# Float32 products of a mixed block in another order: whole-array, half-array and quarter-array products grouped, S5's in-block products moved ahead of its scan

## The chip, the core and the metric

The kernel runs on one core of a Trainium2 chip. The metric is the device time of one launch in microseconds, as the median of several launches. TensorE does the matrix products; VectorE, ScalarE and GpSimd do the rest; SyncE's queue (SP) issues the DMA transfers.

## The reference

Two transformer-like blocks on a sequence of 512 tokens and a width of 1024, all in float32. The first block (two layers of attention and gated products) isn't touched. The second block first mixes its input by three branches whose gated sum goes on, and the change lies in this mix:

```python
def rwkv7_mix(...):      # 8 heads of 64
    def step(S, inp):
        r_t, w_t, k_t, v_t, kk_t, a_t = inp
        sa = jnp.einsum('bhvk,bhk->bhv', S, -kk_t)
        S = (S * w_t[:, :, None, :] + sa[..., None] * (kk_t * a_t)[:, :, None, :]
             + v_t[..., None] * k_t[:, :, None, :])
        return S, jnp.einsum('bhvk,bhk->bhv', S, r_t)

def s5_mix(...):         # 32 groups of 16 channels, 64 complex states each
    _, _, s_re, s_im = lax.associative_scan(_complex_affine_combine, elems, axis=1)
    y = (einsum('blgn,gcn->blgc', s_re, c_re) - einsum('blgn,gcn->blgc', s_im, c_im) + d * uf)
    ...                  # gelu, and a gate by y @ w_glu

def gla_mix(...):        # 4 heads, chunks of 64 tokens
    att = where(mask, einsum('bhncd,bhnsd->bhncs', q_dec, k_inv), 0.0)
    o = einsum('bhncs,bhnse->bhnce', att, v)
    u = einsum('bhncd,bhnce->bhnde', k * exp(b_last - b), v)
    ...                  # S_prev: the state before each chunk, by a scan over chunks
    o = o + einsum('bhncd,bhnde->bhnce', q_dec, S_prev)
```

After the mix come a product with w_out, a cross attention and a convolutional feed-forward part, which are not touched.

## The kernel before

The large projections (x by a weight matrix) are computed as three products of rounded halves: `L282`, `L283` and `L284` in the helper `mm3`, with results in banks called `ps_mm`. Weights come by DMA as `wraw`, ScalarE casts the upper part `wh` at `L312`, and VectorE forms the lower part `wl` at `L314`. Each is one record in the trace. The small products of the mix are plain float32, and each takes two records, since the array passes over them twice. Their banks are called `ps_ch` (RWKV) and `ps_si` (S5 and GLA).

A tensor with 128 channels holds two heads of 64, one in rows 0 to 63 (`UP`) and one in rows 64 to 127 (`DOWN`). A product thus uses the whole array (128 rows by 128 columns, written 128*128 in the profile), a row half (64*128), a column half (128*64) or a quarter (64*64).

RWKV is done in chunks of 64 tokens for four tiles `t` of two heads, in the order 2, 3, 0, 1. `rwkv_a` makes gates and decays (with two products of rank 64 at its start). `rwkv_lower` makes a triangular matrix (`L1482`); its in-chunk inverse, for all four tiles together, is made by `rwkv_invert`, a chain of 30 steps on VectorE (`L1504`, `L1505`), whose result is copied (`L1512`) and goes through DRAM (`L1516`, `L1517`, read back at `L1472`). `rwkv_b` continues with `L1541` and `L1551`, and then

- E and F, per head e: four whole-array products (`L1630`) and four column-half products (`L1631`), one of each in turns into one bank, then the evacuation of that bank;
- G and h, per half of a chunk pair: 24 quarter products (`L1654` to `L1656`) in one bank, heads in turns.

S5 runs in two halves of eight group pairs. Each half makes its injection (`L2105`), rotates and scans it on VectorE and GpSimd (`L2111` to `L2125`), and then, for each group pair, adds two in-block products (`L2147`, matrices `mid`) and four products with the scan's result (`L2151`). The results go to DRAM (`L2092`) and come back for the gated output (`L2165`, then the products by `w_glu`).

GLA runs for two pairs of heads `j`: projections q (evacuated at `L1762`), k (`L1767`) and v, the state updates u (`L1791`), the in-chunk scores (`L1804`), and the output o, per head four products over whole blocks (`L1814`), each followed by two row-half products with the state (`L1817`).

Every part is a Python generator. `yield x` tells the code that builds the program how much TensorE work, in microseconds by its own reckoning, the step has issued, or, as a negative number, how long the next step has to wait for other engines. The builder then puts in projection products and steps of other parts (`kit.fill`), and so sets the order on every engine's queue. A change in a `yield`, or in what stands between two, moves work nearby.

## Time and profile before

| | |
|---|---|
| median of 3 runs | 2738.64 us (2735.85 to 2743.93) |
| profiled execution, its own time | 2742.08 us |
| its span, first to last instruction | 2740.3 us |
| TensorE busy | 2630.8 us, 96 % |
| VectorE, ScalarE, GpSimd busy | 58 %, 43 %, 19 % |
| mean granted TensorE clock | 0.968 |
| second block's mix | 1526 to 2197 us |

The profile was taken in one execution, so its rows add up to its own time. A share of busy time is a mean over stages with different limits. The granted clock is that of TensorE, as a part of 2.4 GHz; a mean between 0.5 and 1 is a mixture of the two levels, 1.2 and 2.4 GHz. The time from one record's start to the next one's says more of what a product costs than its busy time, as products overlap.

### The profile page before, as it was taken

The numbers are of one execution on the slowest core, as the hardware profiler recorded it, in microseconds if no ns is written. First come the engines' busy times: TensorE is split into PE (matmuls) and PEld (weight loads), VectorE is DVE, ScalarE is ACT, GpSimd is POOL, SyncE is SP. The second block draws the span as 40 slices with busy tenths as digits, with TensorE's granted clock in tenths as the row PEclk, the third lists the DMA queues.
The fourth block names the chain that finished last, engine by engine and source line by source line (L and its number), as shares of the span: only waits on it lengthen the run. The fifth ranks groups of instructions, "written<-read, shape, count | busy, mean of one in ns | idle before, by whom it ended". The sixth has DMA issues, their size and how long they took to land. (4 is left out here: it accounts for less than half of the span.)

```text
span 2740.3 us, 37093 instructions
## 1 busy us (share of the span) xinstructions
PE 2630.8 (96%) x13432; PEld 2124.6 (78%) x13432; DVE 1594.6 (58%) x3076; ACT 1182.4 (43%) x2209; POOL 519.7 (19%) x439
## 2 busy tenths in 40 slices
PE   8999999999999998999999889799999999999998
PEld 6668778888776787887877667677878788888886
DVE  5686654344457867966345667635453656774673
ACT  4576543233445755332333231425223445543443
POOL 5325021011210121243112331111130300100001
PEclk9999999999999999999999998799989999999999
DMA  4112223333422131334434343422212433233332
GB/s 153 36 50 90 61 89 93 100 99 91 128 72 62 55 101 55 116 118 139 142 89 135 108 171 107 108 70 83 66 44 72 119 116 102 81 97 95 100 93 70
DMA packets 172520, 258.51 MB, mean 94 GB/s; under 512 B 42528, under 2 KB 60832, under 8 KB 172320
## 3 DMA queue, kind: packets, MB, share of 16 engines
q1 hardware_dynamic: 172336, 256.13, 30.4%
q8 instruction: 106, 1.74, 0.3%
q14 instruction: 78, 0.64, 0.1%
HBM read 234.04 MB, written 22.15 MB: 93 GB/s over the span
## 5 line engine op out<-in xcount | busy, mean ns | idle before, releaser
L312 ACT CAST wh<-wraw 128x512 fp32r<-128x512 f32 (+1 forms) x777 | 473.4, 613 | 920.9 <-PE ps_mm L283 646.1
L314 DVE TENSOR_TENSOR wl<-wraw,wh 128x512 fp32r<-128x512 f32 (+1 forms) x691 | 488.1, 709 | 346.0 <-ACT wh L312 334.0
L282 PE MATMUL ps_mm<-xs,wh 128*128 128x512 f32 x1544 | 626.7, 406 | 8.9 <-ACT wh L312 7.9
L284 PE MATMUL ps_mm<-xs,wl 128*128 128x512 f32 x1544 | 615.6, 399 | 7.7 <-DVE wl L314 6.9
L283 PE MATMUL ps_mm<-xs,wh 128*128 128x512 f32 x1544 | 616.0, 399 | 2.0 <-DVE xs L264 1.9
L282 PEld LDWEIGHTS ps_mm<-xs,wh 128*128 128x128 f32 x1544 | 295.6, 191 | 76.4 <-ACT wh L312 8.5
L284 PEld LDWEIGHTS ps_mm<-xs,wl 128*128 128x128 f32 x1544 | 295.6, 191 | 75.4 <-DVE wl L314 9.6
L283 PEld LDWEIGHTS ps_mm<-xs,wh 128*128 128x128 f32 x1544 | 295.5, 191 | 66.1 <-DVE xs L264 5.7
L448 POOL TENSOR_TENSOR acc<-acc,za 128x512 f32<-128x512 f32 x59 | 82.0, 1389 | 730.4 <-ACT za L444 729.0
L282 PE MATMUL ps_mm<-za,wh 128*128 128x512 f32 x460 | 183.4, 399 | 5.5 <-ACT za L248 5.5
L284 PE MATMUL ps_mm<-za,wl 128*128 128x512 f32 x460 | 182.0, 396 | 4.1 <-DVE wl L314 4.1
L283 PE MATMUL ps_mm<-za,wh 128*128 128x512 f32 x460 | 180.9, 393 | 0.2 <-DVE za L245 0.2
L314 POOL TENSOR_TENSOR wl<-wraw,wh 128x512 fp32r<-128x512 f32 x86 | 112.4, 1316 | 308.5 <-ACT wh L312 303.7
L1193 POOL TENSOR_TENSOR za<-za,za 128x512 f32<-128x512 f32 x44 | 60.0, 1363 | 461.2 <-ACT za L1192 461.2
L284 PEld LDWEIGHTS ps_mm<-za,wl 128*128 128x128 f32 x460 | 87.3, 190 | 24.8 <-DVE wl L314 4.5
L282 PEld LDWEIGHTS ps_mm<-za,wh 128*128 128x128 f32 x460 | 87.5, 190 | 24.4 <-ACT za L248 6.4
L282 PE MATMUL ps_mm<-zb,wh 128*128 128x512 f32 (+1 forms) x284 | 100.6, 355 | 4.4 <-ACT zb L248 4.4
L245 DVE TENSOR_TENSOR za<-ps_tr,za 128x512 fp32r<-128x512 f32 (+3 forms) x152 | 84.6, 558 | 32.9 <-ACT za L248 31.8
L283 PEld LDWEIGHTS ps_mm<-za,wh 128*128 128x128 f32 x460 | 87.2, 189 | 20.4 <-DVE za L245 1.0
L283 PE MATMUL ps_mm<-zb,wh 128*128 128x512 f32 (+1 forms) x284 | 97.3, 343 | 0.1
L284 PE MATMUL ps_mm<-zb,wl 128*128 128x512 f32 (+1 forms) x284 | 97.3, 343 | 0.0
L468 POOL TENSOR_TENSOR rs<-sm,neghalf 128x4 f32<-128x4 f32 (+2 forms) x32 | 44.9, 1404 | 267.4 <-DVE sm L467 267.4
(592 smaller groups left out, 4918.2 us busy)
## 6 DMA issues: line engine op xcount, KB each, us to landing
wraw<-w_gu SPq DMA_DIRECT2D x176, 256.0 KB, 2.7
wraw<-w_dn SPq DMA_DIRECT2D x96, 256.0 KB, 2.6
wraw<-w_up SPq DMA_DIRECT2D x88, 256.0 KB, 2.6
wraw<-w_gate SPq DMA_DIRECT2D x48, 256.0 KB, 2.7
wraw<-w_dn SPq DMA_DIRECT2D x48, 192.0 KB, 2.3
dram<-za SPq DMA_DIRECT2D x26, 256.0 KB, 2.2
zc<-dram SPq DMA_DIRECT2D x26, 256.0 KB, 4.5
wraw<-w_cd SPq DMA_DIRECT2D x24, 256.0 KB, 2.7
```

What stands on the lines that cost most here:

```text
L245: self.nc.vector.tensor_tensor(lo, src, hi.bitcast(F32), op=ALU.subtract)
L282: mm(out, ah, bh, start=start, stop=False, **kw)
L283: mm(out, ah, bl, start=False, stop=False, **kw)
L284: mm(out, al, bh, start=False, stop=stop, **kw)
L312: self.nc.scalar.copy(hl[0], raw)
L314: eng.tensor_tensor(hl[1], raw, hl[0].bitcast(F32), op=ALU.subtract)
L448: self.nc.gpsimd.tensor_tensor(self.acc[0], self.acc[0], sq, op=ALU.add)
L468: self.nc.gpsimd.tensor_tensor(r, ms, self.neghalf[:, :n], op=ALU.pow)
L1193: nc.gpsimd.tensor_tensor(a, a, st["rb"], op=ALU.mult)
```

## The change

The products keep their operands and sums; their order changes, and with it the split into yields.

- `rwkv_a`: the two low-rank products of a tile, one in the upper and one in the lower rows, are issued in turns.
- `rwkv_b`, E and F: both heads get their bank first, the eight whole-array products stand together, then the eight column-half products of the two heads in turns, then both evacuations.
- `rwkv_b`, G and h: one loop over both halves and both heads, so that four quarters stand in turns; the yield between the halves is gone.
- GLA: u's two halves in turns with one yield; o in two banks at once, whole-array products together, then the row halves of the two heads in turns, and one yield of 2 more ahead of the evacuations.
- S5: the in-block products of a half stand ahead of the scan, with their four matrices in the loads made ahead (eleven tiles instead of seven); behind the scan only the scan's products remain, with a yield of 0.5 after every second group pair instead of 1.2 after each.

```diff
@@ -1405,5 +1405,7 @@
         w_up = self.narrow(I["w_up"][:, 0, t * 128 : t * 128 + 128])
-        for rows_, bias, out in ((UP, "w0", sw), (DOWN, "a0", a)):
-            p = kit.bank(CH)
-            kit.mm3(p, [z[rows_] for z in w_up], [z[rows_] for z in self.lora], True, True)
+        ps = [kit.bank(CH) for _ in range(2)]
+        for i, (x, y) in enumerate(((0, 0), (0, 1), (1, 0))):
+            for p, rows_ in zip(ps, (UP, DOWN)):
+                nc.tensor.matmul(p, w_up[x][rows_], self.lora[y][rows_], start=i == 0, stop=i == 2)
+        for p, bias, out in zip(ps, ("w0", "a0"), (sw, a)):
             nc.scalar.activation(out, p, AF.Sigmoid, bias=self.vec(bias, t))
@@ -1624,9 +1626,13 @@
         E, F = kit.f(), kit.f()
-        for e in range(2):
-            p = kit.bank(CH)
-            own, oth = slice(e * 64, e * 64 + 64), slice(64 - e * 64, 128 - e * 64)
+        ps = [kit.bank(CH) for _ in range(2)]
+        for e, p in enumerate(ps):
             for b in range(4):
                 s = slice(b * 128, b * 128 + 128)
-                mm(p[:, s], pair(wu, e, b), bb[e][:, s], start=True, stop=True)
-                mm(p[oth, s], head(st["vt"], e, b), lk[e * 4 + b][:, 128:256], start=False, stop=True, skip_group_check=True)
+                mm(p[:, s], pair(wu, e, b), bb[e][:, s], start=b == 0, stop=True, skip_group_check=True)
+        for b in range(4):
+            s = slice(b * 128, b * 128 + 128)
+            for e, p in enumerate(ps):
+                mm(p[halves[1 - e], s], head(st["vt"], e, b), lk[e * 4 + b][:, 128:256], start=False, stop=True, skip_group_check=True)
+        for e, p in enumerate(ps):
+            own, oth = halves[e], halves[1 - e]
             for b in range(4):
@@ -1645,13 +1651,12 @@
                                     st["pc"][own].unsqueeze(2).broadcast_to([64, 8, 64]), op=ALU.mult)
-        for half in range(2):
-            p = kit.bank(CH)
-            rows_ = slice(half * 64, half * 64 + 64)
-            for b in range(4):
-                for e in range(2):
-                    own = slice(e * 64, e * 64 + 64)
-                    w, u = (pair(wu, e, b)[rows_, o : o + 64] for o in (e * 64, 64 - e * 64))
-                    g_, h_ = p[own, b * 64 : b * 64 + 64], p[own, 256 + b * 64 : 320 + b * 64]
-                    mm(g_, w, head(st["bt"], e, b)[rows_], start=True, stop=True)
-                    mm(h_, head(st["bt"], e, b)[rows_], u, start=True, stop=False)
-                    mm(h_, head(st["kt"], e, b)[rows_], head(st["vt"], e, b)[rows_], start=False, stop=True)
+        ps = [kit.bank(CH) for _ in range(2)]
+        four = [(p, rows_, e) for p, rows_ in zip(ps, halves) for e in range(2)]
+        for b in range(4):
+            g_, h_ = slice(b * 64, b * 64 + 64), slice(256 + b * 64, 320 + b * 64)
+            own_, oth_ = ([pair(wu, e, b)[:, o : o + 64] for e, o in enumerate(os)] for os in ((0, 64), (64, 0)))
+            bt, kt, vt = ([head(st[n], e, b) for e in range(2)] for n in ("bt", "kt", "vt"))
+            for c_, x, y, start, stop in ((g_, own_, bt, True, True), (h_, bt, oth_, True, False), (h_, kt, vt, False, True)):
+                for p, rows_, e in four:
+                    mm(p[halves[e], c_], x[e][rows_], y[e][rows_], start=start, stop=stop)
+        for half, p in enumerate(ps):
             for e in range(2):
@@ -1786,5 +1791,4 @@
             u = [kit.bank(SI) for _ in range(2)]
-            for half in range(2):
-                rows_ = slice(half * 64, half * 64 + 64)
-                for b in range(4):
+            for b in range(4):
+                for half, rows_ in enumerate((UP, DOWN)):
                     for e in range(2):
@@ -1792,3 +1796,3 @@
                            st["kd"][rows_, b * 128 + e * 64 : b * 128 + e * 64 + 64], vb(b, e)[rows_], start=True, stop=True)
-                yield 1.2
+            yield 1.2
             yield -7.0
@@ -1808,11 +1812,13 @@
             yield -3.0
-            for e in range(2):
-                rows_, a = (UP, DOWN)[e], as_[e]
-                o = kit.bank(SI)
+            os = [kit.bank(SI) for _ in range(2)]
+            for e, o in enumerate(os):
                 for b in range(4):
                     w = slice(b * 128, b * 128 + 128)
-                    mm(o[:, w], vb(b, e), a[:, w], start=True, stop=True)
-                    for ch in (2 * b, 2 * b + 1):
-                        w = slice(ch * 64, ch * 64 + 64)
-                        mm(o[:, w], by4(s[ch // 4])[rows_, ch % 4], st["q"][rows_, w], start=False, stop=True, skip_group_check=True)
+                    mm(o[:, w], vb(b, e), as_[e][:, w], start=b == 0, stop=True, skip_group_check=True)
+            for ch in range(8):
+                w = slice(ch * 64, ch * 64 + 64)
+                for o, rows_ in zip(os, (UP, DOWN)):
+                    mm(o[:, w], by4(s[ch // 4])[rows_, ch % 4], st["q"][rows_, w], start=False, stop=True, skip_group_check=True)
+            yield 2.0
+            for o in os:
                 sq, y = kit.f(), kit.f()
@@ -2086,3 +2092,4 @@
             return [kit.load("", src=self.s5_tab[i, half]) for i in range(3)], [
-                kit.load("", src=self.s5_in[o, half * 2 + g]) for o in range(2) for g in range(2)]
+                kit.load("", src=self.s5_in[o, half * 2 + g]) for o in range(2) for g in range(2)], [
+                kit.load("", src=self.s5_mid[:, 16 * half + 4 * g : 16 * half + 4 * g + 4, :].rearrange("p g x -> p (g x)")) for g in range(4)]
 
@@ -2096,3 +2103,3 @@
         for half in range(2):
-            (cs, sn, m8), w_in = ahead
+            (cs, sn, m8), w_in, mids = ahead
             kit.need(*moves[2 * half : 2 * half + 2])
@@ -2114,3 +2121,12 @@
             tt(b, inj[0], sn, op=ALU.mult)
-            yield -4.0
+            yield -2.0
+
+            ps = [kit.bank(SI), kit.bank(SI)]
+            for g in range(8):
+                for e, p in enumerate(ps):
+                    c = (g % 2 * 2 + e) * 128
+                    mm(p[:, g * BLKS : g * BLKS + BLKS], mids[g // 2][:, c : c + 128], block(2 * (8 * half + g) + e),
+                       start=g == 0, stop=True, skip_group_check=True)
+                if g % 4 == 3:
+                    yield 0.9
             pt(x, x, a, op=ALU.add)
@@ -2129,8 +2145,5 @@
                 ahead = half_loads(1)
-            ps = [kit.bank(SI), kit.bank(SI)]
-            mids, cos = {}, {}
+            cos = {}
 
             def out_loads(gp):
-                if gp < 8 * half + 8 and gp % 2 == 0:
-                    mids[gp // 2] = kit.load("", src=self.s5_mid[:, 2 * gp : 2 * gp + 4, :].rearrange("p g x -> p (g x)"))
                 if gp < 8 * half + 8 and gp // 3 not in cos:
@@ -2142,12 +2155,8 @@
                 out_loads(gp + 1)
-                mid, co = mids[gp // 2], cos[gp // 3]
-                p = [z[:, g * BLKS : g * BLKS + BLKS] for z in ps]
-                for e in range(2):
-                    c = (g % 2 * 2 + e) * 128
-                    mm(p[e], mid[:, c : c + 128], block(2 * gp + e), start=True, stop=True)
                 c = gp % 3 * 144 + 16
-                for w, s in zip(co, (sr, si)):
-                    for e, rows_ in enumerate((UP, DOWN)):
-                        mm(p[e][:, 1:], w[rows_, c : c + 128], v8(s)[rows_, g, : BLKS - 1], start=False, stop=True, skip_group_check=True)
-                yield 1.2
+                for w, s in zip(cos[gp // 3], (sr, si)):
+                    for p, rows_ in zip(ps, (UP, DOWN)):
+                        mm(p[:, g * BLKS + 1 : g * BLKS + BLKS], w[rows_, c : c + 128], v8(s)[rows_, g, : BLKS - 1], start=False, stop=True, skip_group_check=True)
+                if g % 2:
+                    yield 0.5
             for e in range(2):
```

The program order shows what the planner makes of it. A row has the line, the operation, output and operands with buffer numbers, and the size; "x4" stands for four alike. Line numbers of the changed kernel are its own: what was `L1630` and `L1631` is `L1631` and `L1635` there, and `L1482` or later lines are shifted by 2 to 13.

On TensorE, E and F of the first tile (t=2), before, for one head (bank 16924); `za` are operands in SBUF:

```order
L1630 MATMUL ps_ch_16924<-za_16620,za_16869 128x128
L1631 MATMUL ps_ch_16924<-za_16521,za_16704 64x128
L1630 MATMUL ps_ch_16924<-za_16620,za_16869 128x128
L1631 MATMUL ps_ch_16924<-za_16521,za_16704 64x128
L1630 MATMUL ps_ch_16924<-za_16620,za_16869 128x128
L1631 MATMUL ps_ch_16924<-za_16558,za_16704 64x128
L1630 MATMUL ps_ch_16924<-za_16620,za_16869 128x128
L1631 MATMUL ps_ch_16924<-za_16558,za_16704 64x128
```

The same place on TensorE in the changed kernel, both heads (banks 17066 and 17067):

```order
L1631 MATMUL ps_ch_17066<-za_16784,za_17039 128x128 x4
L1631 MATMUL ps_ch_17067<-za_16801,za_17052 128x128 x4
L1635 MATMUL ps_ch_17066<-za_16686,za_16898 64x128
L1635 MATMUL ps_ch_17067<-za_16694,za_16898 64x128
L1635 MATMUL ps_ch_17066<-za_16686,za_16898 64x128
L1635 MATMUL ps_ch_17067<-za_16694,za_16898 64x128
L1635 MATMUL ps_ch_17066<-za_16738,za_16898 64x128
L1635 MATMUL ps_ch_17067<-za_16772,za_16898 64x128
L1635 MATMUL ps_ch_17066<-za_16738,za_16898 64x128
L1635 MATMUL ps_ch_17067<-za_16772,za_16898 64x128
```

Whole-array and column-half products alternated, with the other head's eight products elsewhere; now they stand in two blocks for both heads.

On TensorE, the output of S5's second half, before. The rows ahead are GLA's k projection (`ps_mm_16235`), those behind GLA's v:

```order
L284 MATMUL ps_mm_16235<-xs_14112,wl_16232 128x512
L2147 MATMUL ps_si_16006<-x_14829,zc_16008 128x64
L2147 MATMUL ps_si_16007<-x_14829,zc_16008 128x64
L2151 MATMUL ps_si_16006<-zc_15949,zc_16010 128x63
L2151 MATMUL ps_si_16007<-zc_15949,zc_16010 128x63
L2151 MATMUL ps_si_16006<-zc_15952,zc_16012 128x63
L2151 MATMUL ps_si_16007<-zc_15952,zc_16012 128x63
...
L2151 MATMUL ps_si_16006<-zc_15952,zc_16074 128x63
L2151 MATMUL ps_si_16007<-zc_15952,zc_16074 128x63
L282 MATMUL ps_mm_16310<-wh_16288,xs_13673 128x256
```

The same place in the changed kernel; the rows ahead are GLA's gate projection of 16 channels, those behind GLA's q projection (`ps_mm_16169`, weights `wh_16159` and `wl_16160`):

```order
L284 MATMUL ps_mm_16086<-xs_14112,wl_16083 16x512
L2159 MATMUL ps_si_15939<-zc_15903,zc_16016 128x63
L2159 MATMUL ps_si_15940<-zc_15903,zc_16016 128x63
L2159 MATMUL ps_si_15939<-zc_15906,zc_16018 128x63
L2159 MATMUL ps_si_15940<-zc_15906,zc_16018 128x63
...
L2159 MATMUL ps_si_15939<-zc_15906,zc_16058 128x63
L2159 MATMUL ps_si_15940<-zc_15906,zc_16058 128x63
L282 MATMUL ps_mm_16169<-xs_13673,wh_16159 128x512
L283 MATMUL ps_mm_16169<-xs_13674,wh_16159 128x512
L284 MATMUL ps_mm_16169<-xs_13673,wl_16160 128x512
```

The block shrank from 48 products to 32, since 16 in-block products went ahead of the scan, and GLA's q and k projections, which stood ahead of the block, stand behind it.

On VectorE, the end of the inversion, before; `wl` rows are the lower parts of weights (16226 and 16232 for GLA's k, 16289 and 16295 for v):

```order
L1505 TENSOR_TENSOR zc_15749<-zc_15749,zc_15750 128x16x8
L314 TENSOR_TENSOR wl_16226<-wraw_16223,wh_16225 128x512
L1504 TENSOR_TENSOR zc_15750<-zc_15748 128x54
L314 TENSOR_TENSOR wl_16232<-wraw_16229,wh_16231 128x512
L1505 TENSOR_TENSOR zc_15748<-zc_15748,zc_15750 128x6x9
L314 TENSOR_TENSOR wl_16289<-wraw_16286,wh_16288 128x512
...
L1504 TENSOR_TENSOR zc_15750<-zc_15749 128x30
L1505 TENSOR_TENSOR zc_15749<-zc_15749,zc_15750 128x30
L1741 TENSOR_TENSOR zc_16141<-ps_mm_16104,acc_14154 16x512
L314 TENSOR_TENSOR wl_16295<-wraw_16292,wh_16294 128x512
```

The end of the inversion on VectorE in the changed kernel (`wl_16160` and `wl_16166` for GLA's q, 16210 and 16216 for k, 16273 for v; `L1506` and `L1507` are the inversion, `L1746` is what was `L1741`):

```order
L1506 TENSOR_TENSOR zc_15794<-zc_15793 128x30
L1507 TENSOR_TENSOR zc_15793<-zc_15793,zc_15794 128x30
L314 TENSOR_TENSOR wl_16160<-wraw_16157,wh_16159 128x512
L1746 TENSOR_TENSOR zc_16123<-ps_mm_16086,acc_14154 16x512
L314 TENSOR_TENSOR wl_16166<-wraw_16163,wh_16165 128x512
L245 TENSOR_TENSOR zc_16079<-zc_16123,zc_16078 16x512
L314 TENSOR_TENSOR wl_16210<-wraw_16207,wh_16209 128x512
L314 TENSOR_TENSOR wl_16216<-wraw_16213,wh_16215 128x512
L314 TENSOR_TENSOR wl_16273<-wraw_16270,wh_16272 128x512
```

The lower parts of the weights for q and k, which were formed inside the inversion, are formed behind its last step.

## Rows read from the trace of the kernel before

**Rows 1.** The page: span, busy times, and granted clock in 40 slices.
```profile
span 2740.3 us, 37093 instructions
...
PE 2630.8 (96%) x13432; PEld 2124.6 (78%) x13432; DVE 1594.6 (58%) x3076; ACT 1182.4 (43%) x2209; POOL 519.7 (19%) x439
...
PEclk9999999999999999999999998799989999999999
```

**Rows 2.** Windows of the mix: busy us and counts by engine, granted clock, DMA.
```profile
core 0: us, PE busy (x) PEld busy (x) DVE busy (x) ACT busy (x) POOL busy (x), PEclk, DMA share, GB/s
1970.00:2003.00 33.00, 32.27 (x173) 25.57 (x174) 5.99 (x18) 5.76 (x10) 5.61 (x7) 0.64 0.14 42
1700.00:1716.00 16.00, 13.05 (x101) 11.55 (x100) 14.53 (x45) 2.30 (x5) 0.00 (x0) 0.68 0.09 14
1716.00:1750.00 34.00, 22.63 (x138) 19.49 (x137) 15.54 (x21) 15.83 (x25) 6.84 (x5) 0.65 0.49 114
1526.00:2197.00 671.00, 622.08 (x3694) 496.64 (x3693) 366.85 (x674) 233.95 (x400) 156.17 (x126) 0.91 0.31 94
```

**Rows 3.** TensorE's timeline: a whole-array run, and row halves in turns.
```profile
1872.37 0.39 PE L284 MATMUL ps_mm<-xs,wl 128*128 128x512 f32 x1
1872.60 0.27 PE L1574 MATMUL ps_ch<-za,za 128*128 128x128 f32 x1
...
1873.41 0.48 PE L282 MATMUL ps_mm<-xs,wh 128*128 128x512 f32 x1
...
1741.04 1.16 PE L1482 MATMUL ps_ch<-za,za 64*128 64x128 f32 x16
1742.13 0.39 PE L282 MATMUL ps_mm<-wh,xs 128*128 128x256 f32 x1
```

**Rows 4.** TensorE's timeline, E and F of one head, first rows and next.
```profile
1806.52 0.39 PE L1630 MATMUL ps_ch<-za,za 128*128 128x128 f32 x2
1806.84 0.43 PE L1631 MATMUL ps_ch<-za,za 128*64 128x128 f32 x2
...
1809.18 0.43 PE L1631 MATMUL ps_ch<-za,za 128*64 128x128 f32 x2
```

**Rows 5.** TensorE's timeline, GLA's o of one head: first, last and next.
```profile
1809.55 0.38 PE L1814 MATMUL ps_si<-zc,zc 128*128 128x128 f32 x1
...
1813.24 0.38 PE L1817 MATMUL ps_si<-zc,zc 64*128 64x64 f32 x2
1813.56 0.50 PE L282 MATMUL ps_mm<-zc,wh 128*128 128x512 f32 x1
```

**Rows 6.** TensorE's timeline, G and h of one half: first and next.
```profile
1826.34 0.27 PE L1654 MATMUL ps_ch<-za,za 64*64 64x64 f32 x1
...
1828.05 0.50 PE L282 MATMUL ps_mm<-xs,wh 128*128 128x512 f32 x1
```

**Rows 7.** TensorE's timeline, S5's output: one group pair, then the second half.
```profile
1661.39 0.33 PE L2147 MATMUL ps_si<-x,zc 128*128 128x64 f32 x2
...
1662.46 0.50 PE L282 MATMUL ps_mm<-xs,wh 128*128 128x512 f32 x1
...
1700.11 0.55 PE L2147 MATMUL ps_si<-x,zc 128*128 128x64 f32 x4
...
1715.36 0.55 PE L282 MATMUL ps_mm<-wh,xs 128*128 128x256 f32 x1 [2.95 <-DVE zc L1741]
```

**Rows 8.** TensorE's timeline, E and F of another head, first and next.
```profile
1986.90 0.63 PE L1630 MATMUL ps_ch<-za,za 128*128 128x128 f32 x2
...
1992.12 0.47 PE L1654 MATMUL ps_ch<-za,za 64*64 64x64 f32 x2
```

**Rows 9.** VectorE's timeline: the inversion's first and last steps, what follows, S5's read-back.
```profile
1673.98 0.17 DVE L1504 TENSOR_TENSOR zc<-zc 128x14 f32<-128x14 f32 x1
...
1714.36 0.19 DVE L1505 TENSOR_TENSOR zc<-zc,zc 128x30 f32<-128x30 f32 x1
1714.54 0.68 DVE L1741 TENSOR_TENSOR zc<-ps_mm,acc 16x512 f32<-16x512 f32 x1
...
1744.44 0.75 DVE L2165 SCALAR_TENSOR_TENSOR x<-x,vecs,zc 128x512 f32<-128x512 f32 x1 [11.50 <-DMA zc<-dram]
```

**Rows 10.** Waits of TensorE, 1526 to 2198 us: total, times, longest.
```profile
PE ps_ch L510 <- DVE za L498: 9.4, 6, 2.2
PE ps_ch L1551 <- DVE za L1541: 6.2, 2, 4.9
```

## The prediction

> **What bounds the kernel now.** I read the page first: TensorE is busy for 2630.8 of 2740.3 us, and the next engine, VectorE, for 58 % [rows 1]. So time is saved here only if TensorE's own sequence of products gets shorter and nothing that it waits for moves behind. The row of granted clocks on the page is near full but for three slices past the middle (8, 7 and 8 tenths). The program orders of before and after are the same up to the second block's mix and behind it, so only the stretch from 1526 to 2197 us can change. There TensorE is busy 622 of 671 us, at a mean granted clock of 0.91 [rows 2]. Three windows of it stand out by a low clock: 1700 to 1716 us (0.68), 1716 to 1750 us (0.65) and 1970 to 2003 us (0.64). Next I took the timeline of TensorE at the lines that the diff touches, and measured from the start of the first product of a run to the start of what follows it, since busy times of pipelined products overlap. A float32 product is two records there. Last came the waits of TensorE and the timeline of VectorE round the S5 output.
>
> **The change part by part.** First the two prices that a reordering plays with. Eight records of one shape that all use the whole array take 1873.41 − 1872.60 = 0.81 us, 101 ns each; sixteen records that use the two row halves in turns take 1742.13 − 1741.04 = 1.09 us, 68 ns each [rows 3]. Where the shape changes at every product, as in E and F now, sixteen records take 1809.55 − 1806.52 = 3.02 us, 189 ns each [rows 4]. The order of the shapes costs more than the products do.
>
> E and F, four tiles t with two heads each: now 2 × 3.02 = 6.04 us for a t. After: 16 whole-array records at 101 ns (1.62 us) and 16 column-half records in turns; no row shows 128-row column halves of 128 columns in turns, so I bound them by 68 ns (1.09 us) and by 101 ns (no overlap, 1.62 us) and take 68, the row of the same width. With two changes of shape at about 0.1 us (half of what 189 − 101 ns per record comes to over a pair) that is 2.9 us. Gain 3.1 us for a t, 12.6 us in all; bounds 10 and 13.
>
> GLA's o, two j with two heads each: 24 records now take 1813.56 − 1809.55 = 4.01 us [rows 5], 8.02 us for a j. After: 16 whole-array records (1.62 us), 32 half-array records of 64 columns in turns at 68 ns or below (2.18 us), two changes of shape: 3.9 us. Gain 4.1 us for a j, 8.2 us in all; with 31 to 68 ns for the narrow records the bounds are 8 and 10.5.
>
> G and h, eight halves: 48 records take 1828.05 − 1826.34 = 1.71 us, 36 ns each, already in two tiles in turns [rows 6]. After, 96 records run over four tiles. No row has four tiles in turns. If four run no faster than two, nothing is gained; if they run twice as fast, 18 ns, a t gains 1.7 us, 6.8 us in all. I take the middle, 27 ns: 0.8 us for a t, 3.3 us in all. The Trainium skill, page "TensorE: Matmul & The Clock Gate", Part 1, "Wait — 56ns, not 53.3ns?", says that start to start never drops below about 25 ns however small the product; no row here is that low, and by it the term would be at most 1.0 us for a t and the sum some 0.7 us better than mine.
>
> S5's output, sixteen groups: twelve records take 1662.46 − 1661.39 = 1.07 us at full clock [rows 7]. After: four in-block records at 101 ns and eight scan records at 60 ns (between 36 and 68), 0.88 us. Gain 0.19 us, 3.0 us in all; bounds 1.5 and 6. GLA's u and the two low-rank products of rwkv_a change by a few switches between halves: below half a us together, counted at nothing (the same products run, under VectorE's chain).
>
> The sum at full clock: 12.6 + 8.2 + 3.3 + 3.0 = 27 us.
>
> **The clock.** The last run of E/F in the 1970 to 2003 us window takes 1992.12 − 1986.90 = 5.22 us where others take 3.02 [rows 8], and the second S5 half takes 1715.36 − 1700.11 = 15.25 us where eight groups at full clock would take 8 × 1.07 = 8.6 [rows 7]. Both are stretches with small products alone. Shorter, they cost less at either clock; if the clock held, another 2.2 + 6.7 = 9 us would come on top. The three slow windows lose 16 × 0.32 + 34 × 0.35 + 33 × 0.36 = 29 us of full-speed time in all [rows 2]. I count 4 us, half of the first sum, since the dense stretch stays without projection products and the S5 stretch gets a wait (next).
>
> **What moves.** On VectorE the inversion, one chain of 30 steps, runs from 1673.98 to 1714.55 us. The products of the S5 output need nothing of it. In the new order those stand ahead of GLA's q and k projections, and the casts of the q/k weights stand behind the inversion's last step, where four of them stood inside it. So TensorE gets through the shortened S5 output and then has nothing until the inversion ends. It now waits 2.95 us at that place [rows 7]; in the changed kernel I expect 12 to 18 us: in before some 15 us of S5 output stand in front of that end, in after about 48 projection records (48 × 0.23 = 11 us at the spacing of L284 to the next row, 0.23) move behind it. What is late next: q and k evacuations, then the S5 read-back at L2165. That one has its own slack: VectorE stood idle 11.50 us before L2165 on the read-back from DRAM [rows 9], because the loads stood on SP's queue behind the stores of the inverse. In the new order the copies at L1512, and with them those stores, stand behind the gated output, so the loads come before them and this idle time should go. Stall and slack about cancel: I put 0 for it, bounds a loss of 15 (18 us of stall and the 11 us of products at half clock, less the 11.50 us and the wait of 2.95) and a gain of 10. The price paid is that the t=2 state (L1541) begins later, with about 20 us more of other work already behind it.
>
> Waits that the E/F, G/h and o edits expose: both heads now reach the evacuation together, and the products behind them stand closer. TensorE waits now 9.4 us in six places for L498 and 6.2 us for L1541 [rows 10]; two or three more of the size 1 to 2 us in the dense stretch come to 3 us, bounds 0 and 8.
>
> So: −27 − 4 + 0 + 3 = −28 us. The profiled execution took 2742.08 us, 3.4 us more than the median of 2738.64; it goes to 2714, the median to 2711 us.
>
> **Rivals.** Each is measured against the 0.3 % (8 us) that a measurement of this kernel can tell from no change.
> Waits eat it: the shorter products only bring TensorE earlier to VectorE's results, as at L1551 and L510 [rows 10], and the S5 stall costs its 15 us. For: VectorE's chains do not get shorter. Against: in 1526 to 2197 us TensorE is busy 93 % and has projections to put in between [rows 2]. 27 − 15 − 8 − 4 leaves 0 to 8 us: about 2735 us. Chance 0.11.
> The clock recovers: the S5 tail and the dense stretch are shortened so far that the fall is missed, and the stall at the inversion is short: 27 + 9 + up to 10 for the idle time: 2695 us. For: both slow windows begin with long runs of the small products in question. Against: the 1716 to 1750 window is slow because TensorE waits there (22.6 of 34 us busy), and that gets worse. Chance 0.20.
> Slower: the S5 in-block matrices, loaded eleven tiles at once, hold their buffers until the scan; the q/k weights come late through SP and their casts behind the inversion. TensorE then stands still for 18 us, is granted half the clock for the 11 us of q and k and the products of v behind them (another 20 us), and the t=2 tile is left without projections to cover its own chain (10 us). It decides when the loss passes 35 us, since 27 are gained: at 40 us the time is 2750 us. Against: the 11.50 us of idle time in front of L2165 take up the first part. Chance 0.08.
> The change does less than it says: products of the low-rank pair that the scheduler pulls apart, column halves that don't overlap, four tiles no faster than two: E/F 10, o 8, G/h 0, S5 1.5: 19.5 us less the 3 us of waits: 2722 us. It lies within the forecast's own side. Chance 0.15.
>
> **How the numbers follow.** Forecast 2711 us with 0.46, the larger gain 0.20, the smaller 0.15, no change 0.11, slower 0.08. Faster by over 0.3 % holds the first three, 0.81; within 0.3 %, 0.11; slower 0.08. The range reaches from the recovered clock with the bounds of the sums, 2688, to the case of no change, 2736; outside lie the slower case and the tails, about 0.2. The likeliest case alone has 2700 to 2722.
>
> **What would show it.** Sixteen E/F records of one head become a block of 32 for both in 2.8 to 3.0 us; G/h's 96 records take 2.4 to 2.8 us; o's 48 records take 3.6 to 4.0 us; S5's two halves take together under 15 us where they took 25. TensorE waits 12 to 18 us ahead of the q projection for VectorE's cast of the weights, and the idle time of VectorE ahead of the S5 read-back is under 3 us. Wrong would be: products whose spacing stays near 200 ns (then the order of the shapes isn't the cost), or a w_glu start later than in before by more than 5 us (then the S5 move costs more than it gives).

## Result and the profile after

| | before | changed |
|---|---|---|
| median | 2737.51 us (2735.85 to 2743.93, 4 runs) | 2701.05 us (2697.67 to 2706.56, 4 runs) |
| profiled execution, span | 2742.08 us, 2740.3 us | 2697.67 us, 2695.9 us |
| mean granted TensorE clock | 0.968 | 0.978 |

The ratio is 0.9864, with a 95 % interval of 0.9841 to 0.9888: 36.5 us faster by the medians, inside the range of the prediction and 10 us better than its value. The profiled execution of before lies 4.6 us above its median and that of the changed kernel 3.4 us below, so the traces differ by 44.4 us. Some of it is chance: the mix starts at 1526.9 us in the one and at 1524.2 us in the other, behind the same program.

The page of the changed kernel, span, busy times and granted clock in 40 slices:

```profile
span 2695.9 us, 37069 instructions
...
PE 2573.7 (95%) x13432; PEld 2083.8 (77%) x13432; DVE 1594.7 (59%) x3076; ACT 1180.1 (44%) x2208; POOL 518.9 (19%) x439
...
PEclk9999999999999999999999989899999999999999
```

The windows of its mix, as in [rows 2]: the whole mix, the stretch round the inversion's end, the one behind it, and the dense stretch of tile t=0:

```profile
core 0: us, PE busy (x) PEld busy (x) DVE busy (x) ACT busy (x) POOL busy (x), PEclk, DMA share, GB/s
1524.00:2153.00 629.00, 568.68 (x3694) 458.25 (x3692) 366.65 (x674) 232.03 (x400) 155.14 (x126) 0.95 0.33 100
1684.00:1703.00 19.00, 4.45 (x67) 3.95 (x66) 17.25 (x56) 1.59 (x3) 0.00 (x0) 0.73 0.29 55
1703.00:1737.00 34.00, 32.37 (x198) 26.33 (x199) 17.38 (x27) 22.26 (x36) 4.13 (x3) 0.95 0.47 129
1930.00:1963.00 33.00, 31.31 (x269) 27.68 (x269) 12.32 (x25) 13.88 (x27) 6.63 (x6) 1.00 0.18 49
```

The mix takes 629 us for 671. TensorE is busy 53 us less, by the same number of records, and idle 11 us more (60 for 49). The dense stretch is granted the full clock where it had 0.64.

TensorE's timeline in the changed kernel: E and F of both heads (`L1631`, `L1635`), G and h in tile t=2 and in t=0 (`L1660`), o of both heads (`L1817`, `L1821`), each with the row that follows:

```profile
1802.41 0.83 PE L1631 MATMUL ps_ch<-za,za 128*128 128x128 f32 x6
...
1805.31 0.50 PE L282 MATMUL ps_mm<-xs,wh 128*128 128x512 f32 x1
...
1810.98 0.34 PE L1660 MATMUL ps_ch<-za,za 64*64 64x64 f32 x7
...
1812.54 0.50 PE L282 MATMUL ps_mm<-xs,wh 128*128 128x512 f32 x1
...
1962.46 3.34 PE L1660 MATMUL ps_ch<-za,za 64*64 64x64 f32 x96
1965.73 0.50 PE L282 MATMUL ps_mm<-zc,wh 128*128 128x512 f32 x1
...
1762.91 0.72 PE L1817 MATMUL ps_si<-zc,zc 128*128 128x128 f32 x5
...
1766.72 0.50 PE L282 MATMUL ps_mm<-zc,wh 128*128 128x512 f32 x1
```

E and F: 1805.31 − 1802.41 = 2.90 us for two heads, where one took 3.02 [rows 4]. G and h: 1.56 us for 96 records, 16 ns each, where half of them took 1.71 [rows 6]. So it is in t=2 and t=1. In t=3 projection records divide the block (14 records in 0.38 us, then 82 in 1.42). In t=0 it is 3.27 us, and there the program order has one half's bank ahead of the other's, so that two tiles stand in turns and not four. o: 3.81 us for two heads, where one took 4.01 [rows 5].

S5's second half on TensorE, half of its in-block products, its scan products, and the wait behind them; then VectorE at the read-back (`L2174`, which was `L2165`):

```profile
1670.63 0.33 PE L2128 MATMUL ps_si<-x,zc 128*128 128x64 f32 x2
...
1672.34 0.48 PE L282 MATMUL ps_mm<-xs,wh 128*128 128x512 f32 x1
...
1684.00 3.79 PE L2159 MATMUL ps_si<-zc,zc 64*128 64x63 f32 x64
1687.72 0.50 PE L282 MATMUL ps_mm<-xs,wh 128*128 128x512 f32 x1
...
1703.03 0.79 PE L284 MATMUL ps_mm<-xs,wl 128*128 128x512 f32 x1 [14.58 <-DVE wl L314]
...
1724.74 2.74 DVE L2174 SCALAR_TENSOR_TENSOR x<-x,vecs,zc 128x512 f32<-128x512 f32 x4
```

Sixteen in-block records take 1.71 us and 64 scan records 3.72 us, so this half takes 7.1 us where it took 15.25 [rows 7]. Then TensorE waits 14.58 us for a lower part of GLA's q weights behind the inversion, and the 11.50 us for which VectorE waited at the read-back [rows 9] are gone. The first product by w_glu starts at 1733 us, not at 1752; counted from the start of the mix in each trace that is 208.8 for 225.2, 16.4 us earlier.

### The profile page after: what moved, and what is told of

Same layout as the page of the kernel before. It is cut to its first block, busy times and chain, and to the rows that moved or that the text cites. A ratio compares the mean times of both kernels' runs of the same rounds, so it can differ in the third digit from the quotient of the medians.

```text
span 2695.9 us, 37069 instructions
## 1 busy us (share of the span) xinstructions
PE 2573.7 (95%) x13432; PEld 2083.8 (77%) x13432; DVE 1594.7 (59%) x3076; ACT 1180.1 (44%) x2208; POOL 518.9 (19%) x439
## 5 line engine op out<-in xcount | busy, mean ns | idle before, releaser
L312 ACT CAST wh<-wraw 128x512 fp32r<-128x512 f32 (+1 forms) x777 | 473.3, 613 | 886.4 <-PE ps_mm L283 606.9
L314 DVE TENSOR_TENSOR wl<-wraw,wh 128x512 fp32r<-128x512 f32 (+1 forms) x691 | 491.7, 715 | 355.5 <-ACT wh L312 343.5
L314 POOL TENSOR_TENSOR wl<-wraw,wh 128x512 fp32r<-128x512 f32 x86 | 112.5, 1316 | 304.9 <-ACT wh L312 300.1
```

The lines of the kernel that those rows point to most:

```text
L312: self.nc.scalar.copy(hl[0], raw)
L314: eng.tensor_tensor(hl[1], raw, hl[0].bitcast(F32), op=ALU.subtract)
```

## Experiments

All kernels ran in rounds beside the kernel before; each ratio is to it and has its 95 % interval.

**E and F alternated again.** In the changed kernel:

```diff
         for e, p in enumerate(ps):
             for b in range(4):
                 mm(p[:, s], pair(wu, e, b), bb[e][:, s], start=b == 0, ...)
-        for b in range(4):
-            for e, p in enumerate(ps):
-                mm(p[halves[1 - e], s], head(st["vt"], e, b), ...)
+                mm(p[halves[1 - e], s], head(st["vt"], e, b), ...)
```

> The changed kernel with one thing put back: in E and F each whole-array product is followed by its column-half product again, head after head; both banks, the evacuations and the yields stay as in the change, and the order on TensorE is the same up to the first E/F block. If the change of shape at each product is the cost: a block of 32 records takes 6.0 us where the changed kernel has 2.90, four times, so 12.4 us more, 2713 us (2711 to 2719, the upper end if the clock falls in the dense stretch). Rival, that the E/F time is covered by other waits and the gain came from elsewhere: below 2705 us.

Measured: 2710.89 us, ratio 0.9900 (0.9882 to 0.9918): 10 us more than the changed kernel, and the two intervals only just meet. TensorE's timeline of this kernel, the first block and the row behind it:

```profile
1802.53 0.38 PE L1631 MATMUL ps_ch<-za,za 128*128 128x128 f32 x2
1802.84 0.32 PE L1632 MATMUL ps_ch<-za,za 128*64 128x128 f32 x1
...
1808.67 0.50 PE L282 MATMUL ps_mm<-xs,wh 128*128 128x512 f32 x1
```

6.14 us for the 32 records that take 2.90 in blocks. The same products on the same operands and banks cost 192 ns each in the one order and 91 in the other; the change of shape is what E and F paid for. All four blocks run at the full granted clock, 6.14 us three times and 6.25 in the dense stretch. G and h of t=0 take 1.56 us in this kernel, 1.71 less than in the changed one, so the blocks together cost 11.3 us. (The Trainium skill, "TensorEngine Tiling (Array Packing)", Key Properties, says that a change of tiling mode drains the engine; 192 against 91 ns agree with a price at each change.)

**G and h in two tiles.** In the changed kernel, with the loop over the halves outermost:

```diff
-        for b in range(4):
-            ...
-                for p, rows_, e in four:
+        for half in range(2):
+            for b in range(4):
+                ...
+                    for p, rows_, e in four[2 * half : 2 * half + 2]:
```

> The changed kernel with G and h in two tiles in turns (one half's 48 records, then the other's) in place of four; one block, same banks and yields, and the same order elsewhere on VectorE and SP but for two places. If four tiles in turns run faster than two: a block takes 3.3 us where the changed kernel has 1.56, in three of the four tiles, so 5 to 6 us more, 2706 us. Rival, that this time is covered: 2701 us, no difference to the changed kernel.

Measured: 2704.01 us, ratio 0.9875 (0.9856 to 0.9894), 3 us more than the changed kernel and not told apart from it by the intervals. The block itself is told apart; TensorE's timeline of this kernel:

```profile
1816.62 0.45 PE L1661 MATMUL ps_ch<-za,za 64*64 64x64 f32 x8
...
1819.39 0.50 PE L282 MATMUL ps_mm<-xs,wh 128*128 128x512 f32 x1
```

2.77 us for 96 records, 29 ns each, against 1.56 (3.3 was expected). Four tiles in turns do run nearly twice as fast as two; 1.2 us in three of the tiles t make 3.6 us. Before, a block took 2 × 1.71 = 3.42 us, with three products of one head before three of the other; turns after every product gave 0.65 us of the gain and the four tiles 1.21.

**The parts alone.** The changed kernel with `s5_g` as before; the kernel before with the new `s5_g` alone; with the new `rwkv_b` alone; with the new `gla_g` alone; and the changed kernel with `s5_g` and `rwkv_a` as before. (Each takes the whole function from the other kernel; the diff above shows them.)

> The changed kernel with S5's part as before (in-block and scan products mixed per group pair, seven tiles loaded ahead, yields as before). If the gain is the sum of shorter products, S5's share is small: 2 to 5 us lost, 2703 to 2706 us. Rival, that the S5 edit gave most of it through what it moved (the inversion's end, the read-back of S5's result ahead of the inverse's stores, the clock from 1700 us on): 15 to 25 us lost, 2716 to 2726 us.

> The kernel before with the S5 edit alone. Sum of shorter products: 2 to 5 us gained, 2732 to 2736 us. Rival, that what the S5 edit moves is the larger part: 15 to 25 us gained, 2712 to 2722 us. If the two gains depend on each other, this run and the one without the S5 edit don't add up to the 36 us of the whole.

> The kernel before with the E/F and G/h edits alone. By the blocks on TensorE: 12.4 us from E/F and 5.5 us from G/h, 18 us, so 2720 us; with clock regained in the dense stretch down to 2712 us. Rival, that the gain needs the other edits beside it, since waits for VectorE take it up: 2727 us or above.

> The kernel before with the GLA edits (u and o) alone. By the blocks on TensorE: 8.4 us, 2729 us (2724 to 2731). Rival, that o's products come right behind the evacuation of the scores and wait for it: 2735 us or above.

> E/F, G/h and the GLA edits alone, without the S5 edit and without the edit of the two low-rank products. If these two edits give nothing by themselves: 2691 to 2697 us, as without the S5 edit. Rival, that the low-rank edit's shorter block counts: 2698 us or above.

| kernel | median us | ratio | interval |
|---|---|---|---|
| E/F and G/h alone | 2715.58 | 0.9909 | 0.9890 to 0.9928 |
| GLA alone | 2721.28 | 0.9931 | 0.9914 to 0.9949 |
| S5 alone | 2737.97 | 0.9998 | 0.9988 to 1.0008 |
| all but S5 | 2694.09 | 0.9840 | 0.9821 to 0.9859 |
| all but S5 and the low-rank pair | 2693.51 | 0.9843 | 0.9815 to 0.9871 |
| the whole change | 2701.05 | 0.9864 | 0.9841 to 0.9888 |

The parts add up: 0.91 % and 0.69 % make 1.60 %, and all but S5 has 1.60 %. S5's edit alone gives nothing, to within 0.12 %. That is slower than its expectation and its rival said, and the kernel without the edit is faster than both of its own said: neither the shorter products nor what the edit moves shows as a gain. The edit of the low-rank pair gives nothing that is seen either (2693.51 for 2694.09 us). The two versions without the S5 edit have the lowest times of all, but their intervals overlap that of the whole change, so that it costs something is not shown. The E/F and G/h edits gained 25 us (20 to 30) and GLA's 19 us (14 to 24), both more than their blocks became shorter at full clock (18 and 8.4 us). What E/F and G/h gained beyond that was not traced to a cause; GLA's is the next experiment.

**GLA's o alternated again.** In the changed kernel:

```diff
             for e, o in enumerate(os):
                 for b in range(4):
                     mm(o[:, w], vb(b, e), as_[e][:, w], start=b == 0, ...)
-            for ch in range(8):
-                for o, rows_ in zip(os, (UP, DOWN)):
-                    mm(o[:, w], by4(s[ch // 4])[rows_, ch % 4], st["q"][rows_, w], ...)
+                    for ch in (2 * b, 2 * b + 1):
+                        mm(o[:, w], by4(s[ch // 4])[rows_, ch % 4], st["q"][rows_, w], ...)
```

> The changed kernel with one thing put back: in GLA's o each whole-array product is followed by its two row-half products again, head after head; both banks, evacuations and yields stay as in the change. The GLA edits alone gained 19 us where the two blocks of o are only 8.4 us shorter. If the order of the products is all, this costs 8 to 9 us, 2709 us. If the clock follows that order, as much as the edit gained: 2715 to 2721 us. If the edit's other part (both banks ahead of the evacuations, the yields) gave the rest, 2709 us too, with the granted clock as in the changed kernel.

Measured: 2723.66 us, ratio 0.9933 (0.9910 to 0.9956): 19 us lost by the ratios and 22.6 by the medians, as much as the two GLA edits had gained, where the order's own price is 8.4. The windows of exactly the two blocks of o in this kernel, and then in the changed kernel (columns as above):

```profile
1770.70:1781.19 10.49, 10.49 (x49) 8.47 (x48) 3.78 (x6) 2.20 (x4) 0.00 (x0) 0.72 0.21 62
1950.19:1962.29 12.10, 12.10 (x50) 9.89 (x49) 0.58 (x1) 1.18 (x2) 0.00 (x0) 0.60 0.01 1
```

```profile
1762.91:1766.72 3.81, 3.81 (x50) 3.62 (x48) 3.61 (x7) 0.62 (x1) 0.00 (x0) 1.00 0.28 90
1933.16:1936.98 3.82, 3.82 (x49) 3.70 (x49) 0.57 (x1) 0.00 (x0) 0.00 (x0) 1.00 0.02 4
```

The blocks take 22.6 us in place of 7.6. About 8 us each are the order at full clock (48 records at 167 ns, the 4.01 us of [rows 5] twice); the rest is the clock, which falls from full to half while the alternating run goes on, and stays full when the same records stand in blocks. In the first block it is full up to 1775.20 us; behind the two blocks it is still half, from 1781.19 to 1785.40 and from 1962.29 to 1966.40 us. So in o the order of shapes is paid twice, in the spacing and then in the clock. That alternation alone does not bring the fall is shown by E and F alternated again, which kept the full clock; what tells the two apart was not tried. The windows of the kernel with GLA's edits alone agree, at tile t=2 and in the dense stretch (the kernel before has 0.77 from 1790 to 1805 us and 0.84 from 1940 to 2035 us):

```profile
1780.00:1800.00 20.00, 20.00 (x157) 17.34 (x155) 6.45 (x10) 4.86 (x9) 0.00 (x0) 1.00 0.20 67
1930.00:2015.00 85.00, 79.89 (x608) 66.27 (x608) 41.25 (x80) 26.20 (x49) 23.29 (x21) 0.90 0.19 62
```

**Where S5's gain goes.** Three trials at the 14.58 us wait. First the four casts of q and k on GpSimd:

```diff
-            yield from kit.proj_g(I["w_gqk"][j], xs, qk)
+            yield from kit.proj_g(I["w_gqk"][j], xs, qk, eng=None if j else nc.gpsimd)
```

> The whole changed kernel, with the lower parts of the weights of GLA's first q and k (four casts) made by GpSimd, which has nothing to do there, in place of VectorE, where they stand behind the inversion. If the 14.6 us wait of TensorE for these casts is what the S5 edit loses: that wait falls below 2 us, and the time by 7 to 15 us, 2686 to 2694 us. Rival, that VectorE's chain behind the inversion sets the pace there whether q and k are done or not: the wait moves to the next product that needs this chain, and the time stays at 2698 to 2703 us.

Measured: 2704.85 us, ratio 0.9873 (0.9854 to 0.9892). The rival held, with a time 2 us above its range: the wait moved. TensorE's timeline of this kernel has the wait at the small product for GLA's decay, which stands between the products for q in the queue and needs an evacuation behind the inversion:

```profile
1708.15 0.79 PE L282 MATMUL ps_si<-zc,nw 16*128 16x512 f32 x1 [15.79 <-ACT zc L248]
```

The same casts without the S5 edit, as a control:

> The changed kernel without the S5 edit, and the same four casts on GpSimd. There the casts stand inside the inversion and TensorE doesn't wait for them, so if the wait is the cause nothing is to be gained: 2692 to 2697 us, as without the S5 edit. Rival, that the casts help by themselves, by freeing VectorE in its inversion: 2685 to 2690 us, as much gained as in the whole kernel.

Measured: 2699.58 us, ratio 0.9854 (0.9835 to 0.9874); nothing gained there either.

Then that evacuation off VectorE as well:

```diff
-            gd = kit.f()[:16]
-            nc.vector.tensor_tensor(gd, p, self.rb[:16], op=ALU.mult)
-            kit.split(gd, *gk)
+            raw, gd = kit.f()[:16], kit.f()[:16]
+            nc.scalar.copy(raw, p)
+            nc.gpsimd.tensor_tensor(gd, raw, self.rb[:16], op=ALU.mult)
+            nc.scalar.copy(gk[0], gd)
+            nc.gpsimd.tensor_tensor(gk[1], gd, gk[0].bitcast(F32), op=ALU.subtract)
```

> The whole changed kernel, with the four casts of GLA's q and k on GpSimd as before, and besides the evacuation of the 16-channel decay projection (and its split) on ScalarE and GpSimd in place of VectorE. With the casts alone the wait of 15.8 us moved on to the decay product, which needs that evacuation, behind the inversion too. If these two are all that holds TensorE, q and k (11 us) run during the inversion, the wait falls to 4 us or less, and the time to 2690 to 2694 us. Rival, that the inversion's end sets when this stretch ends whatever TensorE has done by then (the evacuations of q and k and the casts for v stand behind it too): the wait moves again, 2698 to 2704 us.

Measured: 2705.81 us, ratio 0.9878 (0.9854 to 0.9902). The one long wait is gone, the largest left there are 5.2 us (for `L314`) and 4.3 us (for the evacuation of q), and the time has not moved. But the idle time is not gone, it is in smaller pieces. The same 42 us in the changed kernel, where TensorE is idle for 16.2 us, and in this one, where it is idle for 13.2:

```profile
1684.00:1726.00 42.00, 25.82 (x182) 20.93 (x182) 29.26 (x74) 14.57 (x24) 4.13 (x3) 0.84 0.45 107
```

```profile
1685.50:1727.50 42.00, 28.77 (x173) 23.24 (x173) 32.98 (x69) 14.76 (x24) 11.50 (x9) 0.80 0.42 108
```

So this trial does not show what the time would be without the stall; no run took it away. It shows that neither VectorE's casts nor that evacuation alone holds TensorE there, as its rival said.

Last, S5's products in blocks, but both behind the scan:

```diff
-            (cs, sn, m8), w_in, mids = ahead
+            (cs, sn, m8), w_in = ahead
...
+            for g in range(8):
+                gp = 8 * half + g
+                out_loads(gp + 1)
+                for e, p in enumerate(ps):
+                    mm(p[:, g * BLKS : g * BLKS + BLKS], mids[gp // 2][:, c : c + 128], block(2 * gp + e), ...)
+                if g % 2:
+                    yield 1.0
```

> The changed kernel with S5's in-block products together but behind the scan, right ahead of the scan's own (loads as in the kernel before, seven ahead; a yield of 1 after every second group). The block order without the move. If the move ahead of the scan is what costs, this keeps the shorter products and loses no more: 2689 to 2693 us. Rival: three of the four casts for q and k still stand behind the inversion here, so the wait stays: 2698 to 2703 us.

Measured: 2700.52 us, ratio 0.9853 (0.9828 to 0.9879), with waits of 12.8 us for `L314` and 8.4 us for `L312` there. The rival held: the wait stays, and the time is neither better than that of the whole change nor told apart from it.

Where the lead goes in the versions with products ahead of the scan shows at the other end of the mix. Three windows of 14 us behind the last tile's product by `center`: in the changed kernel, in the one without the S5 edit, and in the one with S5's blocks behind the scan:

```profile
2068.00:2082.00 14.00, 7.35 (x25) 5.19 (x24) 3.22 (x6) 1.80 (x3) 2.91 (x2) 0.63 0.13 37
```

```profile
2070.00:2084.00 14.00, 13.43 (x63) 10.43 (x62) 6.42 (x11) 4.93 (x8) 3.35 (x2) 1.00 0.36 117
```

```profile
2071.50:2085.50 14.00, 13.42 (x63) 10.43 (x62) 6.43 (x11) 4.93 (x8) 3.36 (x2) 1.00 0.35 116
```

and TensorE's timeline in the first of them:

```profile
2072.95 1.09 PE L510 MATMUL ps_ch<-ident,za 128*128 128x128 f32 x4 [2.54 <-DVE za L498]
...
2078.74 1.65 PE L282 MATMUL ps_mm<-zc,wh 128*128 128x512 f32 x3 [3.42 <-ACT zc L248]
```

With products ahead of the scan, the projections that cover the last tile's chain have been used up before: 25 records in these 14 us against 63, and half the clock for most of it. The 38 records missing there, at 0.23 us each, are 8.7 us of work that was done earlier, and they do not shorten the end: from that product by `center` to the last instruction it is 628.2 us in the changed kernel (2695.9 − 2067.7) and 628.3 without the S5 edit (2698.5 − 2070.2). The kernel with the blocks behind the scan, though, has its 63 records and the full clock there, and is no faster. So missing cover is not what all S5 versions share.

What they share is that RWKV does not go on earlier. VectorE at the last step of the inversion (`L1507`) and the copies of its result (`L1514`), and TensorE's first product by the inverse (`L1576`); the changed kernel first, then the one without the S5 edit:

```profile
1702.19 0.19 DVE L1507 TENSOR_TENSOR zc<-zc,zc 128x30 f32<-128x30 f32 x1
...
1743.81 1.14 DVE L1514 COPY zc<-zc 128x256 f32<-128x256 f32 x4
...
1773.39 0.39 PE L1576 MATMUL ps_ch<-za,za 128*128 128x128 f32 x2
```

```profile
1714.95 0.19 DVE L1507 TENSOR_TENSOR zc<-zc,zc 128x30 f32<-128x30 f32 x1
...
1730.35 3.19 DVE L1514 COPY zc<-zc 128x256 f32<-128x256 f32 x4
...
1772.36 0.38 PE L1576 MATMUL ps_ch<-za,za 128*128 128x128 f32 x2
```

The mix starts at 1524.2 us in the one and at 1527.6 in the other. The inversion ends 9.4 us earlier by that count, the copies come 16.8 us later, amid the gated output (`L2185`), and the product by the inverse starts 249.2 us into the mix for 244.8. It is 248.5 with the blocks behind the scan, 251.8 and 251.3 in the two trials at the wait, and 242.0 in the control. All four tiles of RWKV follow that product, and the last tile's product by `center` comes 543.5 us into the mix in the changed kernel, 542.6 without the S5 edit, 542.2 with the blocks behind the scan and 538.3 in the control. A few us between two traces are chance: the kernels with RWKV's and with GLA's edits alone have 241.1 and 241.4 at that product, where before has 244.9. The lead of 16.4 us at w_glu is thus a lead in work that the tiles do not wait for. This is read from the traces; a kernel with the copies moved ahead on VectorE, or with the projections held back, was not run, so the cause of S5's lost gain stays argued.

## Why the prediction held

**E and F**: 2.9 us a tile forecast, 2.90 in three tiles and 3.01 in the dense one. The step is right, and putting the order back costs the forecast's size, 10 us (11.3 by the blocks) for 12.6.

**o**: 3.9 us forecast, 3.81 and 3.82. Right in its own length; that the alternating order also drags the clock down was put into the clock's term, and there it was much too small.

**G and h**: 2.6 us forecast between bounds of 1.7 and 3.4; 1.56 in two of the tiles t, 0.38 and 1.42 in one that projections divide, 3.27 in the one that kept two array tiles. The four array tiles run beside each other almost in full (1.56 us for the 2.77 of two), and the turns after every product take the time a little under the bound. The Trainium skill's floor of about 25 ns from start to start ("TensorE: Matmul & The Clock Gate", Part 1, "Wait — 56ns, not 53.3ns?") does not hold across four tiles here: the mean is 16 ns. The measurement decides. Single starts lay under that floor in before already, where two array tiles ran (`L1654` and `L1656` both start at 1826.62 us); the forecast looked at the mean of 36.

**S5**: 0.88 us a group forecast; in-block records came at 106 ns and scan records at 58, so 0.9. The two halves take 15.7 us (a wait of 1.83 in the first left out) where they took 25, just over the 15 that were named as a sign. The stall of 12 to 18 us is there with 14.58, the read-back's idle time went as said, and the products by w_glu start 16.4 us earlier. So in the stretch itself stall and slack did not cancel: the slack was the larger. The edit alone still measures 0.9998, and the 3.0 us counted for the shorter products do not show, though the interval reaches to a gain of 3.3 us. The prediction names the reason in passing, that the copies stand behind the gated output and that t=2 begins later, but gives it no term of its own; the traces have RWKV's first product by the inverse 4.4 us later, and the work done ahead missing at the end of the mix. So the 0 came out, but not by the steps that led to it, and is luck.

**The clock** is the term that was mis-sized. 4 us were counted. By the means, 1 − 0.968 of 2740.3 us were 88 us of full-speed time lost, and 1 − 0.978 of 2695.9 us are 59: 28 us came back in the profiled runs. This is not the time gained: the kernel without the S5 edit has a mean of 0.973 in its profiled run and is no slower. By the parts, E/F, G/h and GLA's edits gained 44 us where their blocks became 26 us shorter at full clock, so some 18 us lie beyond the sum of the blocks; for GLA's share the clock is shown as the cause, for the rest it is not. The rival of the recovered clock (2695 us) had the mechanism, and the time lies between it and the forecast; it expected the first long gain in S5's stretch, where it did come (0.65 to 0.95) and was then lost again, while what stayed is, as far as the run with o alternated again shows, what the alternating blocks had cost.

**Waits** were put at 3 us beside a cancelling stall; TensorE's idle time in the mix grew by 11 us, the stall in it.

So that the value came within 10 us of the time is in part a balance of errors: the blocks were summed well (27 us), what came beyond them was counted some 14 us too low, and the whole change gained some 7 us less than all of it but S5, which the intervals do not tell from nothing.

## What to carry to other kernels

Put float32 products of one array shape together and let tiles of disjoint rows or columns stand in turns: a change of shape at every product doubled the time of a block here, four quarter tiles ran nearly twice as fast as two, and in one of two kinds of block the alternating run also lost the clock. A block that is costed at the granted clock of its neighbours can be costed too low; read the clock inside such runs. And when an edit lets a stretch end early, ask whether the chain that ends last starts earlier too, and what the work that moves ahead was covering: here the products by w_glu started 16.4 us earlier, RWKV went on 4.4 us later, and the time stayed the same.

## What the runs showed of the hardware

Quarter tiles in turns over both row halves and both column halves go at 16 ns a record, over one row half at 29 ns. The same 48 records of o are granted the full clock for 3.81 us in blocks, and fall to a mean of 0.60 to 0.72 in 10 to 12 us when whole-array and half-array products alternate, though TensorE is busy all the time in both. Alternating whole-array and column-half products (E and F) kept the full clock over their 6.1 to 6.3 us.
